# A two-layer encoder trunk: the feed-forward's sums moved from GpSimd to VectorE and one DMA, two product sums held in PSUM, a conventional first group

## The chip, the cores and the metric

One core of a Trainium2 chip runs the whole program in one launch. The metric is the device time of one execution in microseconds, as the median of three runs. Engines are named as the profile names them: PE is TensorE, PEld its weight load, DVE is VectorE, ACT is ScalarE, POOL is GpSimd, SP is SyncE.

## The reference, cut to what matters

Two layers. Each normalizes x, projects it for two kinds of attention, adds the attention's output to x, normalizes again and runs a dense feed-forward with a squared ReLU. The change touches the feed-forward alone (x is 512 x 1024, w_ff1 1024 x 4096, w_ff2 4096 x 1024, all float32):

```python
for l in range(DEPTH):                       # 2
    ...                                      # attention part, x = x + mixed @ w_o[l]
    h = rmsnorm(x, mlp_norm[l])
    u = jnp.square(jax.nn.relu(jnp.einsum('bsd,df->bsf', h, w_ff1[l])))
    x = x + jnp.einsum('bsf,fd->bsd', u, w_ff2[l])
return rmsnorm(x, final_norm)
```

## The kernel before, in words

**Precision.** Every float32 operand is split into a rounded part `hi` (ACT, line 116 for weights, 242 and 247 for activations) and the rest `lo` (DVE, lines 132, 243 and 248). `three` multiplies hi by hi, hi by lo and lo by hi (lines 302 to 304), so a product costs three matmuls.

**Seven products for eight.** The feed-forward's 4096 inner features are cut into four groups of 1024, a group into two halves `j` of 512. A matrix product over two by two quarters is done with seven products of sums of quarters instead of eight ("forms": 11, x3, x2, 21, x1, x4, 22). The forms need sums of quarters of the weights, sums of quarters of the activations, and sums of the results.

**First product** (h times w_ff1, `quad_group`). For one half, the four quarters a, b, c, d (11, 12, 22, 21) of w_ff1 are loaded by SP as tiles of 128 x 1024. POOL makes their sums in place (`add`, line 890: e = c + b, b += a, a += e, d += a). A form's weight tile is then split, and 24 matmuls of 256 columns go into one of three PSUM banks X, V, Y. Forms 11, x2, x1 and 22 go on adding in X, x3 and x4 in V, 21 in Y; in between ACT copies X to `m11` (line 1019), V to `v3` (1021) and X to `sx` (1023), and the next form of the same bank waits for that copy. DVE adds Y and m11 (1025), subtracts X and v3 (1030) and adds V and sx (1033); ACT does relu and square (1026, 1027, 1034, 1035, 1045, 1046). POOL makes four sums of 128 x 512 of the squared values (`pool_tt`, line 951), ACT and DVE split them into `sides[j]`, the seven left operands of the second product. The first half of group 0 is conventional: four blocks of 128 features, 24 matmuls of 512 columns each (`block`), whose results `evict_whole` turns into the seven forms with four sums on POOL, while `h_form` makes the sums of h that all later halves use.

**Second product** (u times w_ff2). For each form, two weight tiles of 128 x 1024 (one for each half), 24 matmuls of 512 columns into two banks of a chain X, V or Y. The weight sums are made by DMA: a plain load and then a load by POOL with an add (`fetch` and `grow`, lines 861 and 868). After each form `gather` adds the two banks to y on DVE (line 1073): seven forms, 14 instructions a group.

**Order of the work.** A unit is one weight tile. While PE works on unit i, units up to i + 3 are rounded and split ahead; four split tiles take turns, so the rounding of unit i + 4 waits for PE's last use of unit i. Each engine and each DMA queue takes its instructions in the order in which they were placed; the program's framework sets that order, and `then` hangs loads and sums behind a unit's split. PSUM has eight banks: tags t (2), mm (2), s (3) and o (1).

Of the kernel before, what the change touches and what calls it, by code (L numbers as in the profile page):

```python
# [43 lines left out]
CHAIN1 = {"11": "X", "x3": "V", "x2": "X", "21": "Y", "x1": "X", "x4": "V", "22": "X"}  # L44
# [6 lines left out]
def _unit_list():  # L51
# [5 lines left out]
    for l in range(L):  # L57
# [32 lines left out]
_FIRST = [(l, g, j, q) for l in range(L) for g in range(GROUPS) for j in range(2) if g or j for q in QUADS]  # L90


class _Weights:
# [45 lines left out]
    def do_split(self, n, ahead=None):  # L139
        while self.split < min(n, len(_UNITS)):  # L140
# [4 lines left out]
            if kind != "f":  # L145
                if kind != "s":
                    self.load(_SLOT[i] + 1)
                self.split_part(i, 0, 1024)
                self.rest_of[i] = self.last[1]
            else:  # L150
                for a in (0, 512):
                    self.split_part(i, a, a + 512)
                    if _UNITS[i][3:] == ("x2", 0):
                        self.behind(self.last[0], self.forms)
# [16 lines left out]
def trunk(ctx, tc, opened, xT, w, w2, w1, gfin, lamv, cos, sin, out):  # L171
# [8 lines left out]
    turn = [0]  # L180

    def bank(tag, name):
        if tag == "any":
            tag = ("mm", "s", "s", "mm", "s")[turn[0] % 5]
            turn[0] += 1
        return ps.tile([P, 512], F32, tag=tag, name=name, bufs=banks[tag])
# [151 lines left out]
    for l in range(L):  # L338
# [502 lines left out]
        with ExitStack() as fctx:  # L841
# [31 lines left out]
            groups = [(g, j) for g in range(GROUPS) for j in range(2) if g or j]  # L873
            store_ = {"D": kept[(2, 1)], "E": norms.rearrange("p a t -> p (a t)")}

            def piece(n, role):
                return store_[{"a": "T0", "b": "T1", "d": "D"}.get(role) or ("T2", "E")[n % 2 ^ (role == "e")]]

            def bring(n, role, fresh_tile=False):
                if n == len(groups):  # L880
                    return
                if fresh_tile:
                    k = {"a": "T0", "b": "T1", "c": "T2"}[role]
                    store_[k] = wraw.tile([P, 1024], F32, tag="raw", name=f"{k}_{l}")
                q = {"a": "11", "b": "12", "c": "22", "d": "21"}[role]
                nc.sync.dma_start(piece(n, role), w1[_FIRST.index((l, *groups[n], q))])

            def add(n, to, by, other=None):
                if n < len(groups):
                    nc.gpsimd.tensor_tensor(  # L890
                        out=piece(n, to), in0=piece(n, other or to), in1=piece(n, by), op=ALU.add)

            def first_sums(n):
                add(n, "e", "c", "b")
                add(n, "b", "a")
                if n < len(groups):
                    for form, role in (("11", "a"), ("x3", "e"), ("x2", "a"), ("21", "d"),
                                       ("x1", "b"), ("x4", "d"), ("22", "c")):
                        W.raw[_INDEX[("s", l, *groups[n], form)]] = piece(n, role)
# [7 lines left out]

            bring(0, "d")
            then(("1", l, 1), bring, 0, "a", True)
            for k in (1, 2, 3):  # L910
                then(("1", l, k), skip)
            then(("1", l, 2), bring, 0, "b", True)
            then(("1", l, 3), bring, 0, "c", True)
            then(("1", l, 3), first_sums, 0)
            for n, (g, j) in enumerate(groups):
                then(("s", l, g, j, "11"), add, n, "a", "e")
                then(("s", l, g, j, "x3"), bring, n + 1, "c")
                then(("s", l, g, j, "21"), add, n, "d", "a")
                then(("s", l, g, j, "21"), bring, n + 1, "a")
                then(("s", l, g, j, "x1"), bring, n + 1, "b")  # L920
                if j == 0:
                    then(("s", l, g, j, "x4"), bring, n + 1, "d")
                else:
                    then(("s", l, g, j, "x4"), fetch, g, "21", 1)
                    if g + 1 < GROUPS:
                        then(("f", l, g, "22", 1), bring, n + 1, "d")
                then(("s", l, g, j, "22"), first_sums, n + 1)
# [4 lines left out]
            for g in range(GROUPS):  # L932
                for c in range(GP // 2):
# [4 lines left out]
                    if g + 1 < GROUPS:  # L938
                        then(("f", l, g, "x1", c), fetch, g + 1, "11", c)
                        then(("f", l, g, "x4", c), fetch, g + 1, "x3", c)  # L940
                        if c == 0:
                            then(("f", l, g, "22", c), fetch, g + 1, "21", c)
            W.pools.append(f2)
# [6 lines left out]
            def pool_tt(out, a, b, op):  # L950
                return nc.gpsimd.tensor_tensor(out=out, in0=a, in1=b, op=op)  # L951

            def evict_whole(pt, k):
                pair, which = k // 2, k % 2
                F = kept[(0, pair)].rearrange("p (a t) -> p a t", a=4)
                hi, lo = (e[:, :, pair, :] for e in sides[0])
# [7 lines left out]
                pool_tt(F[:, 1, :], F[:, 1, :], F[:, 0, :], ALU.subtract)  # L964
                pool_tt(F[:, 0, :], F[:, 2, :], F[:, 0, :], ALU.subtract)
# [364 lines left out]
```

## Time and profile before

| | us |
|---|---|
| median of three runs (lowest, highest) | 1236.38 (1234.91, 1239.12) |
| the profiled execution: its time, its span | 1239.4, 1237.6 |
| busy in that span: PE, DVE, ACT, POOL | 1157.1, 973.4, 706.4, 408.9 |
| feed-forward of layer 0, of layer 1 (from the span's start) | 242.1 to 616.6, 854.3 to 1230.1 |
| mean granted TensorE clock | 0.973 |

A busy PE is a PE with matmuls in flight, which overlap; how far the matmuls are apart in a stage says more than that share. In a row of the groups stand: line, engine, operation, out and in, count, then busy us and mean ns of one, then the idle time before. In a row of the windows stand the stretch, its length, and for each engine the busy us and the number of instructions, then the clock granted to PE, the DMA engines' busy share and GB/s. A row of the timeline begins with the start in us and the duration.

### The profile page before, as it was taken

To read this page: it belongs to the slowest core of one execution; us is meant where nothing else is said; L and a number is where in the kernel's file an instruction comes from. 1 tells how busy PE (TensorE), PEld (TensorE's weight loads), DVE (VectorE), ACT (ScalarE), POOL (GpSimd) and SP (SyncE) were. 2 spreads that over 40 slices of the span, in tenths; PEclk is the share of its full clock that TensorE was granted. 3 is DMA by queue.
4 is the path that set the end of the run, shared out by engine and by line. 5 is a ranking of instruction groups with operands and counts; after the bars stand their busy time and mean duration, and the time that the engine had idled before them with its cause. 6 is when DMAs were issued, how large, how long until landed. Compare 5 with 4: busy or idle time off the path is not lost.

```text
span 1237.6 us, 18281 instructions
## 1 busy us (share of the span) xinstructions
PE 1157.1 (93%) x6757; PEld 1017.6 (82%) x6757; DVE 973.4 (79%) x1349; ACT 706.4 (57%) x1227; POOL 408.9 (33%) x353
## 2 busy tenths in 40 slices
PE   9999999988998998999999999999699989889987
PEld 7899898867797798788788998988687877878876
DVE  6897788778677778777878877888868787787777
ACT  6466667556556456456444665656564564564574
POOL 1001333066246256254000013320851651651630
PEclk9999999989998998999999999999899999999999
DMA  7664452437834834827427535413359248248163
GB/s 245 173 176 121 131 154 61 152 123 167 207 100 102 208 99 102 217 73 184 132 68 198 165 115 155 122 64 102 125 132 235 77 102 232 84 97 228 52 126 113
DMA packets 58169, 170.83 MB, mean 138 GB/s; under 512 B 7136, under 2 KB 8416, under 8 KB 58080
## 3 DMA queue, kind: packets, MB, share of 16 engines
q1 hardware_dynamic: 48432, 135.55, 35.2%
q0 software_dynamic: 9216, 33.56, 15.5%
q8 instruction: 53, 0.87, 0.3%
q10 hardware_dynamic: 432, 0.56, 0.1%
q14 instruction: 36, 0.29, 0.1%
HBM read 140.28 MB, written 4.19 MB: 117 GB/s over the span
## 4 chain that ended last, share of the span: by engine, by line
PE 56%; DVE 18%; POOL 8%; issue 6%; ACT 6%; DMA 6%; POOLq 0%; DVEq 0%; SPq 0%; ACTq 0%
DVE wlo L132 8%; POOL x L951 5%; DVE Al L243 4%; PE X L303 4%; PE X L304 4%; PE X L302 4%; DMA q<-in_w 4%; ACT whi L116 2%; PE Y L302 2%; PE Y L303 2%; PE Y L304 2%; PE V L303 1%; PE V L302 1%; PE V L304 1%; PE wo L302 1%
## 5 line engine op out<-in xcount | busy, mean ns | idle before, releaser
L132 DVE TENSOR_TENSOR wlo<-q,whi 128x512 fp32r<-128x512 f32 x192 | 150.7, 827 | 26.7 <-ACT whi L116 26.7
L116 ACT ACTIVATE whi<-q 128x512 fp32r<-128x512 f32 x192 | 110.1, 621 | 82.7 <-PE Y L304 24.9
L243 DVE TENSOR_TENSOR Al<-x,Ah 128x512 fp32r<-128x512 f32 (+1 forms) x70 | 96.5, 1379 | 38.8 <-ACT Ah L242 38.8
L132 DVE TENSOR_TENSOR wlo<-T,whi 128x1024 fp32r<-128x1024 f32 x56 | 93.1, 1663 | 34.8 <-ACT whi L116 34.7
L951 POOL TENSOR_TENSOR x<-x 128x512 f32<-128x512 f32 x56 | 93.0, 1661 | 58.1 <-DVE Al L243 30.1
L302 PE MATMUL X<-whi,Ah 128*128 128x512 f32 x248 | 99.9, 403 | 11.3 <-ACT whi L116 7.0
L116 ACT ACTIVATE whi<-T 128x1024 fp32r<-128x1024 f32 x56 | 59.1, 1056 | 84.1 <-POOL T L890 35.4
L303 PE MATMUL X<-wlo,Ah 128*128 128x512 f32 x248 | 99.0, 399 | 4.1 <-DVE wlo L132 4.0
L116 ACT ACTIVATE whi<-raw 128x1024 fp32r<-128x1024 f32 (+1 forms) x74 | 72.6, 987 | 44.7 <-issue 20.3
L304 PE MATMUL X<-whi,Al 128*128 128x512 f32 x248 | 97.4, 393 | 0.0
L132 DVE TENSOR_TENSOR wlo<-raw,whi 128x1024 fp32r<-128x1024 f32 (+1 forms) x74 | 85.9, 1164 | 13.3 <-ACT whi L116 12.9
L302 PE MATMUL X<-hxh,whi 128*128 128x256 f32 x224 | 70.4, 314 | 24.3 <-ACT x L1019 16.0
L242 ACT ACTIVATE Ah<-x 128x512 fp32r<-128x512 f32 (+1 forms) x70 | 49.8, 712 | 50.3 <-POOL x L951 49.9
L302 PE MATMUL X<-h_hi,whi 128*128 128x256 f32 x224 | 66.6, 297 | 12.5 <-ACT x L1023 12.4
L132 DVE TENSOR_TENSOR wlo<-waves,whi 128x512 fp32r<-128x512 f32 (+1 forms) x60 | 57.1, 972 | 22.4 <-ACT whi L116 22.2
L302 PEld LDWEIGHTS X<-hxh,whi 128*128 128x128 f32 x224 | 48.0, 214 | 28.0 <-ACT x L1019 17.4
L302 PEld LDWEIGHTS X<-whi,Ah 128*128 128x128 f32 x248 | 46.7, 188 | 29.4 <-ACT whi L116 13.9
L868 POOL DMA_DIRECT2D q<-in_w x48 | 42.2, 878 | 85.2 <-DVE wlo L132 84.4
L303 PE MATMUL X<-hxl,whi 128*128 128x256 f32 x224 | 68.5, 306 | 0.0
L304 PE MATMUL X<-hxh,wlo 128*128 128x256 f32 x224 | 68.4, 306 | 0.0
L304 PE MATMUL X<-h_hi,wlo 128*128 128x256 f32 x224 | 66.2, 295 | 0.7 <-DVE wlo L132 0.7
L116 ACT ACTIVATE whi<-waves 128x512 fp32r<-128x512 f32 (+1 forms) x60 | 47.9, 822 | 31.8 <-PE X L304 15.9
(722 smaller groups left out, 4011.0 us busy)
## 6 DMA issues: line engine op xcount, KB each, us to landing
raw<-in_w SPq DMA_DIRECT2D x70, 512.0 KB, 3.7
q<-in_w POOLq DMA_DIRECT2D x64, 512.0 KB, 6.2
q<-in_w SPq DMA_DIRECT2D x48, 512.0 KB, 4.9
T<-in_w SPq DMA_DIRECT2D x36, 512.0 KB, 3.6
waves<-in_w SPq DMA_DIRECT2D x30, 512.0 KB, 5.2
norms<-in_w SPq DMA_DIRECT2D x6, 512.0 KB, 3.6
x<-in_xT SPq DMA_DIRECT2D x8, 256.0 KB, 5.0
park<-x SPq DMA_DIRECT2D x8, 256.0 KB, 2.5
```

The lines of the kernel that those rows point to most:

```text
L116: return self.nc.scalar.activation(o, src, AF.Copy)
L132: self.last = h, nc.vector.tensor_tensor(out=lo[:, a:b], in0=raw[:, a:b], in1=hi[:, a:b].bitcast(F32), op=ALU.subtract)
L242: a = nc.scalar.activation(hi, src, AF.Copy)
L243: nc.vector.tensor_tensor(out=lo, in0=src, in1=hi.bitcast(F32), op=ALU.subtract)
L302: nc.tensor.matmul(pt, ah, bh, start=first, stop=False, skip_group_check=goes_on)
L303: nc.tensor.matmul(pt, ah, bl, start=False, stop=False, skip_group_check=goes_on)
L304: nc.tensor.matmul(pt, al, bh, start=False, stop=last, skip_group_check=goes_on)
L868: nc.gpsimd.dma_start(t, quad(g, q, c), accum_op=ALU.add)
L951: return nc.gpsimd.tensor_tensor(out=out, in0=a, in1=b, op=op)
```

## The change

- **Group 0 is conventional as a whole**: eight blocks instead of four blocks and seven forms. `h_form` is spread over the eight blocks. The tiles for group 0's first weights of the second product are loaded from the start (form 11), and behind blocks 6 and 7 (x3 and 21). In layer 1 the eight turns of x (`forth`) stand behind blocks 4 to 7.
- **POOL computes nothing in the feed-forward.** The sums of squared values (`tt2`) and three of the four weight sums (`add`) are DVE's. The fourth, e = 12 + 22, is made by DMA: a load by SP and a load with an add issued by POOL.
- **Y plus m11 is dropped**: ACT copies X into Y's bank, and form 21 adds its matmuls to it there.
- **V and Y of the second product stay in PSUM over all four groups**: the results of x3 and 21 are added to y once, after the last group (Y in the two t banks, V in the two mm banks). Form x4 gets two banks of its own in groups 0 to 2. The first product's X, V and Y and the X chain take turns in the s and o banks (`temp`).
- **Small things**: the second product's weight tiles are split as one of 1024 columns, not as two of 512; the splits of forms 5, 2 and 6 of both halves stand behind the first-product stage (`rest_of_forms`); SP's and POOL's loads are hung behind other units accordingly.

```diff
         for g in range(GROUPS):
-            for j in range(2):
-                if (g, j) == (0, 0):
-                    units.extend(("1", l, f) for f in range(GP))
-                else:
-                    units.extend(("s", l, g, j, form) for form in FORMS)
+            if g == 0:
+                units.extend(("1", l, f) for f in range(2 * GP))
+            else:
+                units.extend(("s", l, g, j, form) for j in range(2) for form in FORMS)
...
+            def bring(n, role):
...
+                quads = {"a": ("11",), "b": ("12",), "c": ("22",), "d": ("21",), "e": ("12", "22")}[role]
+                for q in quads:
+                    at = w1[_FIRST.index((l, g, j, q))]
+                    if q == quads[0]:
+                        nc.sync.dma_start(spots[role], at)
+                    else:
+                        nc.gpsimd.dma_start(spots[role], at, accum_op=ALU.add)
...
-            def add(n, to, by, other=None):
-                if n < len(groups):
-                    nc.gpsimd.tensor_tensor(
-                        out=piece(n, to), in0=piece(n, other or to), in1=piece(n, by), op=ALU.add)
+            def add(to, by):
+                nc.vector.tensor_tensor(out=spots[to], in0=spots[to], in1=spots[by], op=ALU.add)
...
             for n, (g, j) in enumerate(groups):
-                then(("s", l, g, j, "11"), add, n, "a", "e")
-                then(("s", l, g, j, "x3"), bring, n + 1, "c")
-                then(("s", l, g, j, "21"), add, n, "d", "a")
+                then(("s", l, g, j, "11"), add, "b", "a")
+                then(("s", l, g, j, "x3"), add, "a", "e")
+                then(("s", l, g, j, "x3"), bring, n + 1, "e")
+                then(("s", l, g, j, "21"), add, "d", "a")
                 then(("s", l, g, j, "21"), bring, n + 1, "a")
                 then(("s", l, g, j, "x1"), bring, n + 1, "b")
+                then(("s", l, g, j, "22"), bring, n + 1, "c")
...
-            def pool_tt(out, a, b, op):
-                return nc.gpsimd.tensor_tensor(out=out, in0=a, in1=b, op=op)
+            def tt2(out, a, b, op):
+                return nc.vector.tensor_tensor(out=out, in0=a, in1=b, op=op)
...
                     if form == "11":
-                        nc.scalar.copy(m11, X)
+                        nc.scalar.copy(Y, X)
...
                     elif form == "21":
-                        nc.vector.tensor_tensor(out=F[1], in0=Y, in1=m11, op=ALU.add)
-                        nc.scalar.activation(F[1], F[1], AF.Relu)
+                        nc.scalar.activation(F[1], Y, AF.Relu)
...
-                        pool_tt(F[1], F[1], F[0], ALU.subtract)
-                        pool_tt(F[0], F[2], F[0], ALU.subtract)
-                        pool_tt(F[2], F[2], F[1], ALU.add)
+                        tt2(F[1], F[1], F[0], ALU.subtract)
+                        tt2(F[0], F[2], F[0], ALU.subtract)
+                        tt2(F[2], F[2], F[1], ALU.add)
...
+            def rest_of_forms(form):
+                for j in range(2):
...
+                    if form == "":
+                        split_less(hi[5], lo[5], F[2])
+                    elif form == "11":
                         split(hi[2], lo[2], F[3])
-                        pool_tt(F[3], F[2], F[3], ALU.subtract)
-                        W.forms = split(hi[6], lo[6], F[3])
+                    elif form == "x3":
+                        tt2(F[3], F[2], F[3], ALU.subtract)
+                    elif form == "x2":
+                        split(hi[6], lo[6], F[3])
...
+                    held_on = {"Y": [bank("t", f"Y{l}{r}") for r in range(2)], "V": [bank("mm", f"V{l}{r}") for r in range(2)]}
+                chains = {"X": [temp(k, f"X{l}{g}{k}") for k in (p_, q_)], **held_on}
                 for form in FORMS:
                     total, to = SUMS[form], chains[CHAIN[form]]
-                    opens = form in ("11", "x3", "21")
+                    opens = form == "11" or g == 0 and form in ("x3", "21")
+                    if form == "x4" and not end:
+                        to = [temp(k, f"W{l}{g}{k}") for k in (r_, s_)]
+                        opens = True
...
-                    came = gather(total, to)
+                    if end or form not in ("x3", "21"):
+                        came = gather(total, to)
+                    if g:
+                        rest_of_forms(form)
```

More of the change, by code (lines that the diff above doesn't have):

```diff
@@ L144, in do_split @@
                 break
[L145 to L154, printed above, removed]
+            if kind not in "fs":
+                self.load(_SLOT[i] + 1)
+            self.split_part(i, 0, 1024)
+            self.rest_of[i] = self.last[1]
             self.split += 1
@@ L871, in then @@
                 W.then.setdefault(_INDEX[unit], []).append(lambda: fn(*args))
[L873 to L879, printed above, removed]
+            groups = [(g, j) for g in range(1, GROUPS) for j in range(2)]
@@ L886, in bring @@
[L886 to L899 removed]
+                if role not in spots:
+                    spots[role] = wraw.tile([P, 1024], F32, tag="raw", name=f"first_{role}{l}")
@@ new lines, in bring @@
+                g, j = groups[n]
+                quads = {"a": ("11",), "b": ("12",), "c": ("22",), "d": ("21",), "e": ("12", "22")}[role]
[5 more added lines that the diff above has]
+                        nc.gpsimd.dma_start(spots[role], at, accum_op=ALU.add)
+                for form in serves[role]:
+                    W.raw[_INDEX[("s", l, g, j, form)]] = spots[role]
@@ L942, in trunk @@
                             then(("f", l, g, "22", c), fetch, g + 1, "21", c)
+            for c in range(GP // 2):
+                fetch(0, "11", c)
             W.pools.append(f2)
@@ L1236, in trunk @@
             if last:
-                add, ends, part, whole = last_row(halves)
-                in_order(*first, add, part, store(2, 1, False), whole)
+                add_, ends, piece, whole = last_row(halves)
+                in_order(*first, add_, piece, store(2, 1, False), whole)
                 in_order(*squares, *ends, store(2, 0, True), store_last(halves[1]))
```

122 lines of the change are left out of this document (63 added, 59 removed).

## The prediction

> **What bounds the kernel now.** I read the page's first part, then the feed-forward cut into its stages, then the timeline of one stage, then the waits. "First product" is h times w_ff1 (a half of a group: seven forms of 24 matmuls of 256 columns), "second product" is u times w_ff2 (a whole group: seven forms of 24 matmuls of 512).
>
> ```profile
> span 1237.6 us, 18281 instructions
> PE 1157.1 (93%) x6757; PEld 1017.6 (82%) x6757; DVE 973.4 (79%) x1349; ACT 706.4 (57%) x1227; POOL 408.9 (33%) x353
> ```
>
> PE leads, but the 93% hides what a stage loses. The windows view gives the stages: in each layer four conventional blocks, the seven forms of the other half of group 0, group 0's second product, then both first-product halves and the second product of groups 1 to 3 (layer 0, without two second products; of layer 1 the first three and the last two).
>
> ```profile
> core 0: us, PE busy (x) PEld busy (x) DVE busy (x) ACT busy (x) POOL busy (x), PEclk, DMA share, GB/s
> 242.08:264.39 22.31, 22.31 (x101) 18.33 (x100) 19.69 (x35) 17.44 (x28) 6.08 (x5) 1.00 0.41 135
> 264.39:297.05 32.66, 24.91 (x170) 23.80 (x169) 24.13 (x23) 17.40 (x27) 23.52 (x12) 0.84 0.58 164
> 297.05:343.45 46.40, 41.75 (x171) 32.29 (x170) 31.64 (x38) 24.01 (x40) 17.22 (x14) 0.96 0.80 186
> 343.45:394.28 50.83, 44.32 (x338) 43.51 (x336) 38.44 (x30) 29.52 (x42) 28.23 (x13) 0.93 0.29 86
> 394.28:435.65 41.37, 39.52 (x170) 31.31 (x169) 31.85 (x43) 20.63 (x33) 13.74 (x11) 1.00 0.85 198
> 435.65:485.64 49.99, 44.32 (x338) 43.50 (x336) 40.78 (x32) 28.75 (x40) 27.75 (x13) 0.93 0.30 91
> ...
> 527.00:574.35 47.35, 42.55 (x337) 41.94 (x336) 36.09 (x32) 29.10 (x40) 22.56 (x12) 0.96 0.35 106
> ...
> 854.28:878.25 23.97, 23.97 (x118) 19.98 (x116) 21.37 (x37) 18.34 (x30) 7.70 (x5) 1.00 0.33 100
> 878.25:916.66 38.41, 26.42 (x188) 25.53 (x186) 27.77 (x22) 19.67 (x32) 25.82 (x14) 0.82 0.49 142
> 916.66:958.17 41.51, 39.53 (x170) 31.30 (x169) 31.85 (x43) 20.64 (x33) 13.70 (x11) 1.00 0.85 198
> ...
> 1141.37:1188.72 47.35, 42.54 (x337) 41.93 (x336) 36.24 (x32) 28.95 (x40) 22.27 (x11) 0.96 0.26 73
> 1188.72:1230.10 41.38, 40.03 (x183) 31.83 (x181) 33.12 (x50) 24.85 (x48) 10.71 (x10) 1.00 0.52 111
> ```
>
> What a stage would take without a stall follows from matmuls in flow:
>
> ```profile
> 219.64 0.39 PE L302 MATMUL wo<-mdh,whi 128*128 128x512 f32 x1
> ...
> 241.85 0.39 PE L304 MATMUL wo<-vdh,wlo 128*128 128x512 f32 x1
> ...
> 369.75 0.28 PE L303 MATMUL V<-hxl,whi 128*128 128x256 f32 x1
> ...
> 370.23 0.28 PE L304 MATMUL V<-hxh,wlo 128*128 128x256 f32 x1
> 372.78 0.39 PE L302 MATMUL X<-hxh,whi 128*128 128x256 f32 x1 [2.27 <-ACT x L1019]
> ...
> 373.91 0.41 PE L302 MATMUL X<-hxh,whi 128*128 128x256 f32 x1
> 374.12 0.41 PE L303 MATMUL X<-hxl,whi 128*128 128x256 f32 x1
> ```
>
> From 219.64 to 241.85 are 98 steps, 0.227 us for 512 columns; from 369.75 to 370.23 are four, 0.12 us for 256. So 336 small matmuls need 40.3 us and 168 large ones 38.1. The six first-product stages of groups 1 to 3 take 47.35 to 50.83 us, 296.0 in sum over the six: 54 us are lost. Their second products, 41.37 the first and 41.38 the last of six, lose 20 (249.1 in sum against 228.6), the seven forms of group 0 31 (71.1 against 40.3), its second products 12 (87.9 against 76.2). Together some 117 us; that is what the change can win.
>
> The timeline rows show one loss: at 372.78 PE had waited 2.27 us, and afterwards matmuls go every 0.21 us, which is half clock. The wait is for a copy on ACT, and the ACT and POOL rows tell why the copy is late:
>
> ```profile
> 367.15 3.53 POOL L951 TENSOR_TENSOR x<-x 128x512 f32<-128x512 f32 x2 [3.95 <-ACT x L1035]
> 370.71 1.06 ACT L242 ACTIVATE Ah<-x 128x1024 fp32r<-128x1024 f32 x1 [2.17 <-POOL x L951]
> 372.15 0.58 ACT L1019 COPY x<-X 128x512 f32<-128x512 f32 x1
> ```
>
> ACT takes its work in order; an Ah rounding waits for POOL's sums (L951), and the PSUM copy queued behind it is what PE needs. Over the run:
>
> ```profile
> ACT Ah L242 <- POOL x L951: 49.9, 28, 5.4
> ACT whi L116 <- POOL T L890: 35.4, 8, 5.4
> PE X L302 <- ACT x L1019: 16.0, 7, 2.4
> PE X L302 <- ACT x L1023: 12.4, 6, 3.0
> PE X L302 <- DVE x L1030: 8.3, 11, 1.2
> ```
>
> **The change part by part.** First, what POOL does to DVE:
>
> ```profile
> 384.72 5.32 DVE L132 TENSOR_TENSOR wlo<-q,whi 128x512 fp32r<-128x512 f32 x2
> ...
> 391.17 1.28 DVE L132 TENSOR_TENSOR wlo<-q,whi 128x512 fp32r<-128x512 f32 x2
> ...
> 386.75 2.74 POOL L890 TENSOR_TENSOR T<-T,T 128x1024 f32<-128x1024 f32 x1
> ...
> 364.81 1.21 DVE L132 TENSOR_TENSOR wlo<-T,whi 128x1024 fp32r<-128x1024 f32 x1
> ...
> L132 DVE TENSOR_TENSOR wlo<-T,whi 128x1024 fp32r<-128x1024 f32 x56 | 93.1, 1663 | 34.8 <-ACT whi L116 34.7
> ...
> L243 DVE TENSOR_TENSOR Al<-x,Ah 128x512 fp32r<-128x512 f32 x56 | 67.2, 1201 | 29.1 <-ACT Ah L242 29.1
> L1073 DVE SCALAR_TENSOR_TENSOR y<-X,r,y 128x512 f32<-128x512 f32 x58 | 41.5, 746 | 0.6
> ```
>
> The same pair of subtractions takes 5.32 us while POOL adds and 1.28 us when it does not. I price DVE in the changed kernel at the quiet rows: 1.2 us for 1024 columns, 0.65 for 512. The other bound is the means over the run, 1.66 and 1.20, if they have another cause and stay (rival 3).
>
> *DVE, groups 1 to 3.* Added per half: three sums of 1024 columns (3.6 us) and four of 512 (2.6). Removed per half: Y plus m11 (L1025, 0.65, now ACT copies X into Y's bank and the matmuls go on there: one ACT copy as before). Per group the gathers of "x3" and "21" go (four, 0.75 each) and pairs of 512 splits become one of 1024 (1.28 to 1.2). DVE's whole work per group is then 14 first-product and 14 second-product splits (33.6), six weight sums (7.2), per half 8.3 of evictions, subtractions and small splits (16.6), ten gathers (7.5): 65 us against 78.4 us of unstalled PE. DVE fits, with some 13 us of air; now it is busy 70 us of a 92 us group (38.44 + 31.85).
>
> *Does the order fit inside a group?* I walk it with PE unstalled, t = 0 at the first form, a form every 2.9 us. Four split tiles mean that a form's rounding on ACT starts when the form four before ends. Y's copy of form 11 stands behind one rounding (1.06): done at 4.6, needed by x2 at 5.8. Form x2's copy is done a microsecond before x1 needs it. For "22", DVE must have read X of x1: queued ahead of that are two weight sums, two or three splits and one small one; done at 16, needed at 17.3. In the second half the same read is done at 36.9 and needed at 37.4, DVE being back to back from 20.5 on. In the second product's x2, DVE's gather and both splits are done 2 us early, because no rounding waits for POOL's last sum any more. One new head-of-line wait: the sum b += a waits for two reloads, and splits and evictions stand behind it on DVE. b's reload starts at about 5.1 and 28, and
>
> ```profile
> L868 POOL DMA_DIRECT2D q<-in_w x48 | 42.2, 878 | 85.2 <-DVE wlo L132 84.4
> ...
> raw<-in_w SPq DMA_DIRECT2D x70, 512.0 KB, 3.7
> q<-in_w POOLq DMA_DIRECT2D x64, 512.0 KB, 6.2
> ```
>
> puts it there 4 to 5 us later; up to 11.3 and 33.3 PE does not see it, so a slow landing costs about 1 us in the second half. The sum of 12 and 22 that goes to an accumulating DMA (one load, then 0.9 us on POOL and 6.2 to land, about 11 us) is issued a half ahead, 5 us early at least; POOL has nothing else in front of it. I keep 1.7 us lost per first-product stage (bounds 0.5 and 5, the second being half of today's) and 0.9 per second product (bounds 0.3 and 3.3, today's): 6 x 42.0 = 252 against 296.0, and 6 x 39.0 + 1.5 for the turned columns and the tail = 235.5 against 249.1. That is -44 and -13.6.
>
> *Group 0.* Four more conventional blocks (96 x 0.227 = 21.8) replace seven forms (20.2 of matmuls, but 32.66 and 38.41 us of time): +1.6 per layer in work, less all those stalls. DVE has about 41 us of work in 43.6 (12 splits 14.4, four form splits 4.7, 20 scalings of 256 about 8 and 36 small subtractions and sums of 256 about 12.6, at 0.35 to 0.4 each, an estimate from half the 512 row, the first b sum 1.2); no block's split is late in the walk, since three are made ahead. Layer 1 adds eight times four transposes, 2.2 us of PE. I take 44.2 and 47.0 for the eight blocks (bounds 43.6 and 45.8, and 50 each): 91.2 against 22.31 + 32.66 + 23.97 + 38.41 = 117.4, or -26.2. The second product after it, whose first weights now have their tiles from the start and whose x3 pieces load while blocks 5 to 7 run: 39.6 each (bounds 38.4 and 44), 79.2 against 87.9, -8.7.
>
> Sum: -44 - 13.6 - 26.2 - 8.7 = -92.5. The profiled execution took 1239.4 us (span 1237.6 and 1.8 around it), 3 us above the median of the three timed runs; the forecast is 1239.4 - 92.5 = 1147, rounded up to 1148. All best bounds give -107 (1132), all worst -42 (1197).
>
> Half clock is part of the lost time: one minus PEclk times the stage's length is 5.2 us for 264.39 to 297.05, 3.6 for 343.45 to 394.28, and over all feed-forward stages about 32 us. I take it to follow the gaps of 2 us and more (372.78 above), and the gaps left are near 1 us. [...]
>
> **Rivals.** 1. *The queue wait moves to DVE.* DVE is in order too, and now carries sums that wait for DMA landings. If landings run 3 us late, the X read before "22" is 2 to 3 us late in both halves, PE falls to half clock again, and every term stands at its worst bound: 6 x 45.3 for the first products, second products as today, 100 for the blocks. Time 1197. For: DVE is back to back through the second half. Against: landings of 3.7 us. Chance 0.15.
>
> 2. *The clock stays low though the gaps go*, its windows coming from something else: 32 us stay, 1148 + 32 = 1180. Against: the second-product stages of 41.4 us, which lose 3 us in smaller pieces, have 1.00. Chance 0.05.
>
> 3. *Slower: DVE becomes the bound.* If the stretched times are not POOL's doing, the 1024 sums cost 1.66 us and the 512 ones 1.20 on DVE: 6 x 1.66 + 8 x 1.20 - 4 x 0.75 - 2 x 0.65 = +15 us per group on 70, and if DVE's 22 us of waiting per group stay, a group takes 107 us instead of 92: six times 15, 1239 + 90 = 1329. It decides once DVE's work and waits in a group pass 92 us. Against: 5.32 and 1.28 above. Chance 0.08.
>
> **How the numbers follow.** Forecast 0.70, the rivals 0.15, 0.05, 0.08, and 0.02 that the edits cancel within 0.3% (3.7 us, what a measurement of this kernel can tell from none). Faster 0.90, same 0.02, slower 0.08. The range runs from the best bounds, 1132, to 1197, which takes in rival 2 and half of rival 1: about 0.8.
>
> **What would show it.** Right: POOL has no 128x1024 or 128x512 sums in the feed-forward; DVE's 1024 splits average 1.2 to 1.25 us; first-product stages last 41 to 44 us at PEclk 1.00, second ones 38.5 to 40; the waits on L1019 and L1023 are gone; the eight blocks take 44 to 48. Wrong: wlo rows still at 1.6; PE waiting 2 us before "22" or "x1"; PEclk 0.93 in the first-product stages; a DVE sum of weights idle ahead of a DMA.

## The result and the profile after

The changed kernel takes 1138.05 us (median of four runs, 1137.06 to 1140.21) against 1236.01 before, a ratio of 0.921 with a 95% interval of 0.918 to 0.923. The forecast was 1148 with a range of 1132 to 1197: faster, as forecast, and 10 us below its centre. The profiled execution took 1137.6 us.

The first part of the page after the change, and its chain of waits:

```profile
span 1135.8 us, 17692 instructions
PE 1120.2 (99%) x6613; PEld 992.8 (87%) x6613; DVE 897.8 (79%) x1313; ACT 686.8 (60%) x1115; POOL 151.5 (13%) x237
...
PE 82%; issue 8%; DMA 4%; DVE 3%; ACT 1%; POOL 1%; POOLq 0%; DVEq 0%; ACTq 0%
```

PE's share rose from 93 to 99%: outside its busy time stand 15.6 us instead of 80.5, and the span shrank by 101.8 us. DVE has the same 79% of a shorter span although it took over POOL's sums: its busy time fell by 75.6 us. POOL's fell by 257.4 us. The chain is PE for 82% of the span.

The stages in the windows view: the eight blocks and the second product of group 0, then first and second products of groups 1 to 3 in layer 0; of layer 1 the blocks and the last second product.

```profile
240.28:284.30 44.02, 44.02 (x198) 36.43 (x196) 39.74 (x68) 32.78 (x53) 4.61 (x5) 1.00 0.69 193
284.30:322.38 38.08, 38.08 (x170) 31.53 (x168) 22.42 (x24) 21.64 (x27) 5.23 (x6) 1.00 0.92 243
322.38:365.34 42.96, 40.56 (x338) 40.36 (x337) 32.00 (x34) 29.50 (x39) 3.61 (x5) 1.00 0.62 165
365.34:403.44 38.10, 38.10 (x170) 31.54 (x169) 29.22 (x33) 18.95 (x22) 5.13 (x6) 1.00 0.87 215
403.44:443.76 40.32, 40.32 (x338) 40.31 (x337) 33.20 (x36) 28.85 (x37) 3.65 (x5) 1.00 0.61 164
...
800.16:846.92 46.76, 46.76 (x222) 38.86 (x221) 39.91 (x68) 34.86 (x59) 4.44 (x5) 1.00 0.67 184
...
1084.55:1127.77 43.22, 41.11 (x183) 33.04 (x181) 33.31 (x43) 23.87 (x38) 4.46 (x6) 0.96 0.47 105
```

Before, a first-product stage lost 7 to 10.5 us; now the stage at 403.44 takes 40.32 us for 336 matmuls that need 40.3, and the second product at 365.34 takes 38.10 for 38.1. At these steps (0.12 us for 256 columns, 0.227 for 512) nothing is left to gain in such a stage without fewer matmuls. PEclk is 1.00 in every feed-forward stage but the last. DVE works 33.2 + 29.2 = 62.4 us in the group at 365.34 to 443.76 (the walk had 65).

VectorE's groups, kept apart by shape (busy time and mean ns):

```profile
L130 DVE TENSOR_TENSOR wlo<-q,whi 128x1024 fp32r<-128x1024 f32 x96 | 116.7, 1222 | 56.7 <-ACT whi L114 53.6 <-PE xT L1088 2.6 <-PE V L298 0.5
L940 DVE TENSOR_TENSOR x<-x 128x512 f32<-128x512 f32 x48 | 33.1, 689 | 15.0 <-ACT x L1041 14.3
L237 DVE TENSOR_TENSOR Al<-x,Ah 128x512 fp32r<-128x512 f32 x48 | 32.9, 685 | 1.2 <-ACT Ah L236 1.2
L888 DVE TENSOR_TENSOR first_b<-first_b,first_a 128x1024 f32<-128x1024 f32 x12 | 14.7, 1222 | 20.7 <-DMA first_b<-in_w 20.7
```

The split of 1024 columns is at 1222 ns (mean 1663 for the T pieces before), that of 512 activation columns at 685 (1201 before). The last row shows the only weight sum that waits for a transfer, 20.7 us over the run; the sums of squared values (L940) wait 14.3 us for ScalarE's squares.

What is left of PE's waiting has two places. This is the timeline of the first (start, duration, engine, instruction, and in brackets the idle time before it and what ended it):

```profile
336.19 1.23 DVE L888 TENSOR_TENSOR first_b<-first_b,first_a 128x1024 f32<-128x1024 f32 x1 [5.62 <-DMA first_b<-in_w]
...
341.47 0.68 DVE L1036 SCALAR_TENSOR_TENSOR x<-X,x 128x512 f32<-128x512 f32 x1
...
342.20 0.39 PE L296 MATMUL X<-hxh,whi 128*128 128x256 f32 x1 [2.40 <-DVE x L1036]
```

The reload of b landed at 336.19, 13.8 us into the stage. DVE stood 5.62 us, and the read of X (L1036) that PE needs before "22" came 2.4 us late. It is the prediction's "new head-of-line wait", with its slack: the walk said that PE sees nothing up to 11.3 us, and 13.8 less 11.3 is 2.5. The stage at 885.88 and the one at 1043.57 lose 0.9 and 0.7 us at the same form.

The second place is the last stage:

```profile
1086.47 0.63 ACT L1243 ACTIVATE x<-x 128x512 f32<-128x512 f32 x1 [2.72 <-DMA x<-in_gfin]
...
1098.94 1.06 ACT L114 ACTIVATE whi<-q 128x1024 fp32r<-128x1024 f32 x1 [3.65 <-DMA q<-in_w]
...
1100.05 0.51 PE L296 MATMUL X<-whi,Ah 128*128 128x512 f32 x1 [1.32 <-ACT whi L114]
```

ScalarE stands in order behind the scaling of the last norm's vector, which waits for its DMA; a late weight piece follows 12 us later, and half clock after that (PEclk 0.50 for 3.41 us, 0.96 over the stage). This stage loses 4.7 us against the 38.5 that its matmuls need in flow (an estimate, a little more than the 38.1 of 168 steps of 0.227 us, for its last form is cut finer).

### The profile page after: what moved, and what is told of

It reads as the page before. It is cut to its first block, busy times and chain, and to the rows that moved or that the text cites. A ratio compares the mean times of both kernels' runs of the same rounds, so it can differ in the third digit from the quotient of the medians.

```text
span 1135.8 us, 17692 instructions
## 1 busy us (share of the span) xinstructions
PE 1120.2 (99%) x6613; PEld 992.8 (87%) x6613; DVE 897.8 (79%) x1313; ACT 686.8 (60%) x1115; POOL 151.5 (13%) x237
## 4 chain that ended last, share of the span: by engine, by line
PE 82%; issue 8%; DMA 4%; DVE 3%; ACT 1%; POOL 1%; POOLq 0%; DVEq 0%; ACTq 0%
PE X L296 6%; PE X L297 6%; PE X L298 6%; PE wo L296 3%; PE wo L297 3%; PE wo L298 3%; PE f L298 3%; PE f L296 3%; PE f L297 3%; PE V L298 2%; PE V L297 2%; PE V L296 2%; DVE wlo L130 2%; PE Y L298 2%; PE Y L297 2%
## 5 line engine op out<-in xcount | busy, mean ns | idle before, releaser
L130 DVE TENSOR_TENSOR wlo<-q,whi 128x1024 fp32r<-128x1024 f32 x96 | 116.7, 1222 | 56.7 <-ACT whi L114 53.6
L114 ACT ACTIVATE whi<-q 128x1024 fp32r<-128x1024 f32 x96 | 100.8, 1056 | 91.7 <-DMA q<-in_w 28.0
L130 DVE TENSOR_TENSOR wlo<-waves,whi 128x1024 fp32r<-128x1024 f32 x40 | 48.9, 1222 | 17.1 <-ACT whi L114 17.1
L114 ACT ACTIVATE whi<-waves 128x1024 fp32r<-128x1024 f32 x40 | 42.3, 1057 | 32.7 <-PE X L298 16.6
L296 PE MATMUL X<-hxh,whi 128*128 128x256 f32 x192 | 54.6, 285 | 3.4 <-DVE x L1036 3.4
L297 PEld LDWEIGHTS X<-wlo,Ah 128*128 128x128 f32 x248 | 47.0, 190 | 10.4 <-DVE wlo L130 1.1
L298 PEld LDWEIGHTS X<-whi,Al 128*128 128x128 f32 x248 | 47.0, 189 | 9.9
L297 PE MATMUL X<-h_lo,whi 128*128 128x256 f32 x192 | 54.3, 283 | 0.0
L296 PE MATMUL f<-h_hi,whi 128*128 128x512 f32 x128 | 50.3, 393 | 0.0
L298 PE MATMUL f<-h_hi,wlo 128*128 128x512 f32 x128 | 49.9, 390 | 0.0
```

Of the source, the lines that this page charges most:

```text
L114: return self.nc.scalar.activation(o, src, AF.Copy)
L130: self.last = h, nc.vector.tensor_tensor(out=lo[:, a:b], in0=raw[:, a:b], in1=hi[:, a:b].bitcast(F32), op=ALU.subtract)
L296: nc.tensor.matmul(pt, ah, bh, start=first, stop=False, skip_group_check=goes_on)
L297: nc.tensor.matmul(pt, ah, bl, start=False, stop=False, skip_group_check=goes_on)
L298: nc.tensor.matmul(pt, al, bh, start=False, stop=last, skip_group_check=goes_on)
```

## The experiments

**e1, the sums back on GpSimd.** The changed kernel with its weight sums and squared-value sums on POOL; the rest of the change stays.

```diff
-                nc.vector.tensor_tensor(out=spots[to], in0=spots[to], in1=spots[by], op=ALU.add)
+                nc.gpsimd.tensor_tensor(out=spots[to], in0=spots[to], in1=spots[by], op=ALU.add)
...
-                return nc.vector.tensor_tensor(out=out, in0=a, in1=b, op=op)
+                return nc.gpsimd.tensor_tensor(out=out, in0=a, in1=b, op=op)
```

> The changed kernel with its sums put back on POOL: the three weight sums of 1024 columns and the sums of squared values (each with both inputs in SBUF); the conventional group 0, the sum by DMA and the product sums held in PSUM stay. Theory A (the gain is POOL's arithmetic: ACT's queue waits for its results and DVE's two-input instructions are stretched while it runs): the first-product stages of groups 1 to 3 go back from 40.3 to 43.0 us to 47 to 50, the second ones from 38.1 to about 40, so 1138 + 6 x 8 + 6 x 2 = about 1198 us, 1180 to 1215. Theory B (the gain is structure: group 0 and the sums held in PSUM): below 1160 us.

Measured 1184.8 us (ratio to before 0.957, 0.955 to 0.958), theory A. Waits of this run (in total, times, longest), and then one of VectorE's groups:

```profile
ACT Ah L236 <- POOL x L940: 49.5, 23, 3.8
...
PE X L296 <- ACT Y L1026: 18.2, 6, 3.6
```

```profile
L130 DVE TENSOR_TENSOR wlo<-first_b,whi 128x1024 fp32r<-128x1024 f32 x12 | 35.2, 2935 | 5.1 <-ACT whi L114 5.1
```

The first row is the 49.9 us of the kernel before, almost to the number: an Ah rounding waits for POOL's sum, and PE for the PSUM copy queued behind it. The split of b's weights, beside a long weight sum, takes 2935 ns. The six first-product stages take 284.0 us in sum (246.0 in the changed kernel, 296.0 before). Of the second products, group 0's in layer 0 takes 42.3 us and the others 38.1 to 39.2 where no layer ends, less than the 40 expected. Against the kernel before, e1's profiled execution is 54.8 us shorter, and 30 of these are in group 0 (its first product and its second), 12 in the first products and 12 in the second products of the other groups. That is where the rest of the change pays.

**e2, the kernel before with its sums on VectorE**, the other half of the change:

```diff
-                    nc.gpsimd.tensor_tensor(
+                    nc.vector.tensor_tensor(
...
-                return nc.gpsimd.tensor_tensor(out=out, in0=a, in1=b, op=op)
+                return nc.vector.tensor_tensor(out=out, in0=a, in1=b, op=op)
```

> The kernel before with one edit: its four weight sums a half and its sums of squared values run on DVE instead of POOL; seven forms in group 0 and all gathers stay. Theory A: the waits for POOL and the stretched DVE instructions go, DVE has 4.9 + 2.6 us more work a half, first-product stages of 42 to 45 us and second ones of 39 to 40, group 0 wins some 20: 1236 - 6 x 6 - 6 x 2 - 20 = about 1168 us, 1150 to 1185. Theory B: 1215 us or more.

Measured 1168.6 us (0.943, 0.940 to 0.945), theory A. With e1 this makes a square: the move of the sums alone is worth 5.7%, the rest of the change alone (held product sums, conventional first group, e by DMA) 4.3%, both 7.9%, not 10. I take it that they cure some of the same stalls; which ones was not tried. The square is not quite exact: the sum e is on DVE in e2 and made by DMA in e1. Rival 3 falls here too; DVE with all sums on it has

```profile
L132 DVE TENSOR_TENSOR wlo<-T,whi 128x1024 fp32r<-128x1024 f32 x56 | 68.4, 1222 | 15.8 <-ACT whi L116 15.7
L243 DVE TENSOR_TENSOR Al<-x,Ah 128x512 fp32r<-128x512 f32 x56 | 38.4, 685 | 0.1
```

where before had 1663 and 1201 on the same instructions.

**e3, sums on GpSimd that nobody reads.** The changed kernel, plus eleven POOL sums of 128x512 in each half's seven forms, into a tile that is not used; their operands are the two split weight tiles.

```diff
                     u = W.next("s")
+                    for n_ in range(0, 1024 if form in ("11", "x3", "21", "22") else 512, 512):
+                        hi_, lo_ = (e[:, n_ : n_ + 512].bitcast(F32) for e in u)
+                        nc.gpsimd.tensor_tensor(out=junk, in0=hi_, in1=lo_, op=ALU.add)
```

> The changed kernel with eleven sums of 128x512 on POOL added to each first-product half of groups 1 to 3, from a form's split weight tiles to a tile nobody reads: no engine waits for their results, but POOL reads SBUF while DVE subtracts. If the neighbour alone stretches DVE (mean of a 1024 split in those stages from 1.22 to 1.6 us or more), the stages lengthen by 2 to 7 us each and the time is 1150 to 1180 us. If only waiting for POOL's results cost time, DVE's means stay at 1.22 and the time is within 4 us of 1138.

Measured 1225.9 us (0.990, 0.988 to 0.992): by the ratios the neighbour alone costs 86 us, well beyond the 1180 expected. A group of VectorE and that of the unread sums; PE's longest wait, which is for DVE's read of X; one stage; and rows of its timeline:

```profile
L130 DVE TENSOR_TENSOR wlo<-waves,whi 128x1024 fp32r<-128x1024 f32 x40 | 69.9, 1747 | 7.0 <-ACT whi L114 7.0
L1021 POOL TENSOR_TENSOR junk<-whi,wlo 128x512 f32<-128x512 f32 x132 | 243.4, 1844 | 91.1 <-DVE wlo L130 84.6
```

```profile
PE X L296 <- DVE x L1041: 56.7, 12, 6.0
```

```profile
418.31:475.57 57.26, 45.78 (x338) 45.17 (x337) 49.40 (x39) 29.14 (x37) 40.49 (x25) 0.85 0.49 123
```

```profile
417.57 6.83 POOL L1021 TENSOR_TENSOR junk<-whi,wlo 128x512 f32<-128x512 f32 x3 [1.23 <-DVE wlo L130]
418.48 1.40 DVE L1084 SCALAR_TENSOR_TENSOR y<-X,r,y 128x512 f32<-128x512 f32 x2
...
419.80 1.21 DVE L130 TENSOR_TENSOR wlo<-waves,whi 128x1024 fp32r<-128x1024 f32 x1
...
421.05 2.21 DVE L888 TENSOR_TENSOR waves<-waves,first_a 128x1024 f32<-128x1024 f32 x1
423.18 2.31 DVE L130 TENSOR_TENSOR wlo<-first_b,whi 128x1024 fp32r<-128x1024 f32 x1
```

DVE's busy time in the stage is 49.40 us against 33.20, and the stage 57.26 against 40.32: 16 us more of DVE, 17 more of stage, for results that nothing depends on. For 11.5 of the 17 PE has no matmuls, and for 5.5 its matmuls take longer (45.78 us busy instead of 40.32, at a clock of 0.85). ScalarE, which writes the split tiles anew, waited for the unread sums 2.8 us in the whole run, so it is not such waits that cost the time. In the timeline the two gathers at 418.48, which read PSUM and one SBUF tile, take 0.70 us each beside POOL (their mean in the changed kernel is 744 ns), while of the three instructions with two SBUF operands that follow the split at 419.80 takes 1.21, but the sum at 421.05 and the split at 423.18 take 2.21 and 2.31 instead of 1.22. Here VectorE did become what PE waits for, as in rival 3, but through POOL's work and not without it. The second products of groups 1 to 3, which have no such sums, stay at 38.1 to 38.3 where no layer ends.

**e8 and e9, fills instead of sums.** e3 leaves open whether VectorE lost its time to POOL's reading of two SBUF operands or to any work on POOL. e8 replaces each unread sum by a sum of four columns, to keep it at its place, and four fills:

```diff
-                        hi_, lo_ = (e[:, n_ : n_ + 512].bitcast(F32) for e in u)
-                        nc.gpsimd.tensor_tensor(out=junk, in0=hi_, in1=lo_, op=ALU.add)
+                        hi_, lo_ = (e[:, n_ : n_ + 4].bitcast(F32) for e in u)
+                        nc.gpsimd.tensor_tensor(out=junk[:, 0:4], in0=hi_, in1=lo_, op=ALU.add)
+                        for _ in range(4):
+                            nc.gpsimd.memset(junk, 0.0)
```

> As the kernel with the unread sums on GpSimd, at the same places, but each 128x512 sum (two operands read from SBUF, 1.84 us) is replaced by a sum of four columns and four fills of the same tile with zero (nothing read), some 2 us by the one fill of 128x384 in the profile of before (422 ns). Their result is not used. Theory A (VectorE is stretched by GpSimd's reading of SBUF): 1136 to 1150, and the weight split of 1024 columns stays at 1.22 to 1.27 us. Theory B (any GpSimd work at these places stretches VectorE or holds its queue by waits): 1190 to 1230, with the split at 1.5 us or more.

Measured 1235.7 us (0.997, 0.995 to 0.998). The time is theory B's, a little above its range; the durations are theory A's. So the run was badly sized and its time decides nothing. A group and a wait of it:

```profile
L130 DVE TENSOR_TENSOR wlo<-waves,whi 128x1024 fp32r<-128x1024 f32 x40 | 49.0, 1224 | 58.6 <-ACT whi L114 58.5
```

```profile
ACT whi L114 <- POOL junk L1021: 115.7, 58, 4.4
```

POOL had more work than a stage is long (2 x 28.9 us in 40.3), and ScalarE, which must not overwrite a weight tile that POOL still has to read, waited for it. e9 has one small sum and four or two fills to a form:

```diff
+                    hi_, lo_ = (e[:, 0:4].bitcast(F32) for e in u)
+                    nc.gpsimd.tensor_tensor(out=junk[:, 0:4], in0=hi_, in1=lo_, op=ALU.add)
+                    for _ in range(4 if form in ("11", "x3", "21", "22") else 2):
+                        nc.gpsimd.memset(junk, 0.0)
```

> The run with fills on GpSimd gave GpSimd more than it could do: eleven sums of four columns (459 ns) and 44 fills (543 ns) to a pass of seven forms are 28.9 us of work in a pass of 20.2, so ScalarE came to wait for GpSimd (115.7 us), and that time answered nothing about contention. Here a pass has seven of the small sums and 22 fills, 15.2 us, as against eleven sums of 1.84 us (20.3 us as they were stretched) in the kernel with the unread sums. Their result is not used. Theory A (GpSimd's reading stretches VectorE, its writing does not): 1136 to 1150, first-product stages of 40.3 to 42 us, the 1024-column split at 1.22 us. Theory B (GpSimd's work at these places costs by waits, whatever it reads): 1165 or more, stages above 45 us.

Measured 1143.0 us (0.923, 0.920 to 0.927), theory A, within half a per cent of the changed kernel. The slowest of its first-product stages, and some rows of its timeline:

```profile
402.21:444.61 42.40, 40.78 (x337) 40.41 (x336) 33.12 (x36) 28.03 (x37) 29.34 (x54) 1.00 0.55 155
```

```profile
421.13 1.21 DVE L130 TENSOR_TENSOR wlo<-norms,whi 128x1024 fp32r<-128x1024 f32 x1
421.22 1.18 POOL L1020 TENSOR_TENSOR junk<-whi,wlo 128x4 f32<-128x4 f32 x1
...
422.46 2.29 POOL L1022 MEMSET junk<- 128x512 f32 x4
422.86 1.21 DVE L130 TENSOR_TENSOR wlo<-first_a,whi 128x1024 fp32r<-128x1024 f32 x1
424.83 0.20 POOL L1020 TENSOR_TENSOR junk<-whi,wlo 128x4 f32<-128x4 f32 x1
```

POOL is busy 29.3 us of the stage and DVE 33.1, as without it. The sum of four columns takes 0.20 us alone and 1.18 beside a split: it ends when the split ends (422.40 and 422.34). The fills take 527 ns in the mean of the run, and the split at 422.86 takes 1.21 us beside them; the splits of waves, which e3's sums stretched to 1747 ns in the mean, are at 1220 in e9 and 1222 in the changed kernel.

**e11 and e12, one kind of sum at a time** back on GpSimd, of e1's two edits the second alone (squared values) and the first alone (weights).

> The changed kernel with the sums of the squared values alone put back on GpSimd (seven or so of 128x512 to a stage); the weight sums stay on VectorE. With both kinds back it was 1185, 47 us above the changed kernel. Theory A (what costs is the chain: ScalarE stands in order behind the sum that it splits next, 49.5 us of such waits with both kinds back, and holds the weight splits): 1165 to 1185 here. Theory B (what costs is the weight split stretched to 2.9 us beside the long weight sums): 1140 to 1155 here.

> The other half: the three weight sums of a pass (128x1024) alone on GpSimd, the squared values' sums on VectorE. Theory A (the chain of the squared values costs): 1140 to 1155 here. Theory B (the stretched weight split costs): 1160 to 1185 here. Should both halves alone stay under 1150, neither theory holds by itself and the two wait for each other.

Measured 1170.6 us (0.944, 0.942 to 0.947) and 1159.3 us (0.936, 0.934 to 0.938). Of the times, e11's is in A's range; e12's lies between the two ranges, four above A's and under one below B's. By the ratios the squared values cost 29 us and the weight sums 19, together 48, and both at once (e1) 45: nearly a sum. Two waits and a split of e11, and then two waits and a split of e12:

```profile
ACT Ah L236 <- POOL x L940: 46.0, 22, 3.1
PE X L296 <- ACT x L1030: 16.2, 6, 3.0
L237 DVE TENSOR_TENSOR Al<-x,Ah 128x1024 fp32r<-128x1024 f32 x12 | 25.7, 2143 | 4.1 <-ACT Ah L236 4.0
```

```profile
ACT whi L114 <- POOL first_a L888: 22.3, 7, 3.6
ACT whi L114 <- POOL waves L888: 15.9, 6, 3.2
L130 DVE TENSOR_TENSOR wlo<-norms,whi 128x1024 fp32r<-128x1024 f32 x12 | 31.3, 2610 | 1.1 <-ACT whi L114 1.1
```

In e11 the chain of ScalarE behind POOL's squared values is there nearly whole (46.0 of 49.5 us). In e12 it is gone, but ScalarE's weight roundings wait 38.2 us for POOL's weight sums (4.0 in the changed kernel, for DVE's). And both have stretched splits: 2143 ns in e11 for 1024 activation columns (1219 in the changed kernel), 2610 in e12 for a weight split (1217). So the two runs price the two kinds of sums. They do not separate the two mechanisms, in-order waits and stretching, as their theories had it; how the 45 us of e1 divide between these stays open.

**e4, the held sums undone**: x3 and 21 gathered in each group, x4 on V's banks again.

```diff
-                    opens = form == "11" or g == 0 and form in ("x3", "21")
-                    if form == "x4" and not end:
+                    opens = form in ("11", "x3", "21")
+                    if False:
...
-                    if end or form not in ("x3", "21"):
-                        came = gather(total, to)
+                    came = gather(total, to)
```

> The changed kernel with the product sums of x3 and 21 added to y after every group, as before (12 gathers of 0.75 us more on DVE per layer, x4 on V's banks again, which must be read first). Theory A: DVE has some 14 us of air in a group, so 1138 to 1144 us. Theory B: the held sums are a main part of the gain, 1155 us or more.

Measured 1142.4 us (0.923, 0.921 to 0.926 against the changed kernel's 0.918 to 0.923): theory A, and hardly to be told from the changed kernel. Once the sums are off POOL, the two held product sums are worth 7 us at most. The conventional group 0 was not undone by itself.

**e7, the sum of 12 and 22 on VectorE** instead of the accumulating DMA:

```diff
-                quads = {"a": ("11",), "b": ("12",), "c": ("22",), "d": ("21",), "e": ("12", "22")}[role]
+                quads = {"a": ("11",), "b": ("12",), "c": ("22",), "d": ("21",), "e": ()}[role]
...
+                if role == "e":
+                    nc.vector.tensor_tensor(out=spots["e"], in0=spots["b"], in1=spots["c"], op=ALU.add)
```

> The one sum that the change gave to a DMA, e=12+22, is made on VectorE instead, 12 more sums of about 1.22 us, each queued behind the transfer of c, which is issued only one form earlier. Theory A (a sum on VectorE is only as good as the transfer it waits for: the queue stands 5 to 6 us in each of the six passes that follow a first-product stage, and the splits behind it stand too): 1150 to 1175, with TensorE waiting for split weights at the start of the first-product stages. Theory B (VectorE is idle a fifth of the time and the queue has slack): 1138 to 1144.

Measured 1156.5 us (0.933, 0.931 to 0.935): A's time, not A's wait. The sum's row among VectorE's waits, and a stage:

```profile
DVE norms L885 <- DMA first_c<-in_w: 9.3, 7, 1.7
```

```profile
405.62:448.04 42.42, 40.81 (x338) 40.41 (x336) 33.95 (x37) 28.08 (x37) 1.74 (x2) 1.00 0.40 112
```

No wait of 5 to 6 us: 1.7 at most. Each first-product stage instead loses 2 to 3 us in small pieces, and most second products about 0.9, the one that ends layer 0 3.0. I read it as the longer chain from c's landing over the sum and its rounding to PE; that was argued from these rows and not tried by itself.

**e5, e6 and e10, what the changed kernel still loses.** e6 makes b = 12 + 11 by an accumulating DMA too; e10 moves the scaling of the last norm's vector two forms later; e5 does both.

```diff
-                quads = {"a": ("11",), "b": ("12",), "c": ("22",), "d": ("21",), "e": ("12", "22")}[role]
+                quads = {"a": ("11",), "b": ("12", "11"), "c": ("22",), "d": ("21",), "e": ("12", "22")}[role]
...
-                then(("s", l, g, j, "11"), add, "b", "a")
...
-                    if end and last and form == "x2":
...
+                    if end and last and form == "21":
...
```

> Two edits on the changed kernel. The sum b=12+11 is made by an accumulating DMA, as e=12+22 already is, so that no vector instruction waits for a weight transfer early in a stage; and the scaling of the last norm's vector, which stands ahead of the end of layer 1 on ScalarE, is moved two forms later. Theory A (what the changed kernel still loses is the wait of the vector queue for first_b, 2.7 us of idle TensorE at 339.5, 0.9 at 903 and 0.7 at 1060.7, and some 4.7 us at the end of layer 1 behind ScalarE's 2.7 us wait for that vector): 1138 less 4 to 9, so 1129 to 1134. Theory B (the lost time moves to the accumulating DMAs, which then queue on GpSimd three where there were two): 1136 to 1142. The last second-product stage of layer 1 shows the second edit alone: 40.2 us before it, 36 to 38 by A.

> The first of those two edits alone: b=12+11 by an accumulating DMA, the twelve vector sums of 1222 ns gone. Theory A (the vector queue's wait for first_b is what TensorE loses 2.7, 0.9 and 0.7 us to): 1134, and the three gaps at 339.5, 903 and 1060.7 gone from the first-product stages, whose longest is then 41 us. Theory B (the wait only changes its transfer): 1137 to 1141.

> The changed kernel with the scaling of the last norm's vector alone moved from form x2 to form 21 of the last second-product stage. Theory A (the 4.7 us lost there are ScalarE's wait for that vector and what comes of it): 1138 less 3.5 to 4.5, so 1133 to 1135, the stage at 36 us and the rest as in the changed kernel. Theory B (the run with both edits gained as much there and gave it back in the second products, and so would this one): 1137 to 1139.

Measured 1137.3 us for e5 (0.918, 0.916 to 0.920), 1141.0 for e6 (0.921, 0.919 to 0.923), 1136.8 for e10 (0.918, 0.916 to 0.920). The medians of e5 and e10 lie above theory A's ranges; the kernel before ran some 3 us slower on those chips, and by the ratios both gain 0.3%, 3.6 us, with intervals that overlap that of the changed kernel. e5 and e6 ran on one chip and differ in the scaling alone: 3.7 us, with ranges that do not touch. That edit gains what A said; e10's last stage takes 39.5 us instead of 43.2, not the 36 expected, which is less than its matmuls need. The b edit gains nothing, as B said. e5's second product of group 0, its first product of group 1 and its last stage, and then two of its waits:

```profile
284.95:326.17 41.22, 38.89 (x169) 31.38 (x168) 24.06 (x27) 22.23 (x28) 5.70 (x7) 1.00 0.94 239
326.17:366.49 40.32, 40.32 (x338) 40.31 (x337) 30.12 (x32) 29.73 (x39) 5.38 (x7) 1.00 0.79 200
...
1087.97:1127.16 39.19, 38.81 (x183) 31.98 (x181) 32.84 (x43) 23.04 (x37) 4.57 (x6) 1.00 0.51 115
```

```profile
POOL first_b L883 <- DMA first_b<-in_w: 89.7, 10, 10.2
ACT whi L114 <- DMA q<-in_w: 51.8, 22, 4.1
```

All six first-product stages are at 40.3 us: the three gaps are gone, as A said. But POOL's queue now stands up to 10.2 us until b's first part has landed, the accumulations for the second product stand behind it, ScalarE's wait for those pieces grows to 51.8 us (28.0 in the changed kernel), and the second products that end no layer lose 0.5 to 3.1 us each. The wait moved from one in-order queue to another. e10 is by its ratio the best version, but hardly to be told from the changed kernel.

## Why the prediction was right, and where it was off

**The bound and the mechanism** were right. Undoing the move (e1) brings back ACT's wait for POOL and the late PSUM copies; doing it alone (e2) brings DVE's durations to those priced; and e3 with e9 show that POOL's sums of two SBUF operands, not its being busy, stretched DVE (the splits of waves at 1747 ns beside the sums, at 1220 beside the fills). What is not shown is how much of the move's gain is the stretching and how much the waits. The quiet rows as a price were right: 1.22 us for 1024 columns; for 512 it was 0.69, not 0.65.

**The terms.** First products: 246.0 us for the six against 252 forecast. Second products: 236.0 against 235.5. Blocks with layer 1's transposes: 91.6 against 91.2. Group 0's second products: 76.3 against 79.2. The difference is 8 us, most of the 10.

**The step that was off** is "I keep 1.7 us lost per first-product stage and 0.9 per second product", and the 1.5 us kept in each second product of group 0. Four of six second products and both of group 0 lost nothing, and the six first-product stages lost 4 us together instead of 10. The second products' sum came out right by two errors: nothing lost in four of the stages, and 4.7 us in the last, where I had not seen the scaling of the norm's vector (L1243) ahead of ScalarE's queue; moving it (e10) brings 3.7 of them back. That this sum was right is luck.

**Rival 1** occurs, by its mechanism and with the slack of the walk, but in three of the twelve halves, and for 0.7 to 2.7 us. Its premise, landings 3 us late, holds at 336.19, where two other loads of 512 KB were under way (8.2 us from issue to landing); the median for b over the run is 4.8. Two of the prediction's signs of being wrong appear there: PE waiting 2 us before "22", and a weight sum idle ahead of a DMA. The walk put the risk into the second half; it came in the first. e10 had the same wait again, 14.2 us into the stage, and lost 2.8.

**Rival 2** falls: PEclk is 1.00 in every stage but the last, so the 32 us of half clock went with the gaps. That half clock follows gaps of 2 us and more, as the prediction took it, held in the kernel before (all ten gaps of 2.26 to 9.44 us in its feed-forward), but not in the changed kernel (2.40 us, last section). **Rival 3** was refuted for the changed kernel by its own rows.

## What to carry to other kernels

Work on an otherwise idle engine is not free: price it by what the instructions beside it cost while it runs, and by who stands in order behind its result; here 243 us of unread sums on an idle GpSimd cost 86 us. When a wait is removed from one in-order queue by handing its work to another, list what is queued behind it there (e5 took three gaps away and paid for them in the second products). A walk of the order by hand, with the time at which each input must have landed, was good to a tenth of a microsecond where it could be compared (b's sum: 2.5 us late by the walk, 2.4 measured), whereas the blanket allowance laid on top of it was the largest error.

## What the runs showed of the hardware

In these runs length alone does not say whether a gap brings half clock (PEclk 0.50). In the kernel before, 2.27 us of waiting were followed by it; in the changed kernel 2.40 us were not, but 1.32 us in its last stage were; and e10, at the same form as the 2.40 us, has

```profile
343.10 0.39 PE L296 MATMUL X<-hxh,whi 128*128 128x256 f32 x1 [2.82 <-DVE x L1036]
```

and paid 4.6 us in that stage for a gap of 2.8.

The granted clock in the traces tells them apart. In the profiled executions of the kernel before and of the changed one, its changes between full and half clock lie whole multiples of 3.41 us apart (to 2 ns). Each of these rows is one piece of that grid, two of the changed kernel and then two of e10:

```profile
337.30:340.71 3.41, 2.51 (x21) 2.30 (x20) 3.38 (x4) 0.61 (x1) 0.00 (x0) 1.00 0.29 68
340.71:344.12 3.41, 1.92 (x16) 1.92 (x17) 3.41 (x6) 1.26 (x2) 0.00 (x0) 1.00 0.21 85
```

```profile
340.32:343.73 3.41, 0.63 (x5) 0.63 (x6) 3.38 (x5) 1.06 (x1) 0.00 (x0) 1.00 0.45 154
343.74:347.15 3.41, 3.41 (x18) 3.41 (x18) 2.33 (x4) 2.12 (x2) 0.00 (x0) 0.50 0.49 154
```

In e10 the gap falls into one piece, in which PE is busy for 0.63 us, and the next piece is at half clock. In the changed kernel a border of the grid cuts the gap, PE is busy for 2.51 and 1.92 us of the two pieces, and the clock stays. The gap of 2.27 us left 1.14 us busy in its piece; that of 1.32 us, with another of 0.76 behind it, left 1.34. In the two executions, before and changed, 18 pieces at full clock were followed by half clock, and PE was busy for at most 1.66 us of each; in those followed by full clock it was busy for 1.92 us or more. So in these runs a gap cost half clock where it took about half of one piece or more, and the same gap fell differently on the grid: against the span's start the grid lies 0.39 us earlier in e10 than in the changed kernel.
